# Attention in one decoder block: probabilities turned in 32x32 blocks on VectorE, values on eight places of TensorE's array, three engines in a written order

## The chip, the cores and the metric

The kernel runs on one core of one Trainium2 chip. The metric is device time in microseconds (us), from the start of the execution to its end; the time of a kernel is the median of three runs.

## What is computed

One layer of a hybrid decoder on x of 512 tokens by 1024 channels, in float32. An RMS norm and one input projection feed a sparse-attention mixer, an RWKV-7 mixer and two merge gates; each mixer's result is projected, both are added under sigmoid gates, one more projection and the residual follow, then a gated MLP with a short causal convolution. The change concerns the attention mixer: 8 query heads of 64 in 2 groups (g) that share keys and values, with three branches. At this size all eight blocks of 64 keys are selected and the window of 512 covers all earlier keys, so the selected and the window branch are both plain causal attention, each with keys and values of its own.

```python
s_c = einsum('bsgrd,bcgd->bgrsc', q, kc) + bias_c          # 31 compressed keys
p_c = masked_softmax(s_c, dist_c >= 0, axis=-1)
o_cmp = einsum('bgrsc,bcgd->bsgrd', p_c, vc)
...
sc = einsum('bcgrd,bgcnld->bgrcnl', q_b, k_sel) + bias     # selected keys
p = masked_softmax(sc, mask, axis=(-2, -1))
o_slc = einsum('bgrcnl,bgcnld->bcgrd', p, v_sel)
...
sc = einsum('bqgrd,bkgd->bgrqk', q_b, kw) + bias           # window keys
p = masked_softmax(sc, mask, axis=-1)
o_win = einsum('bgrqk,bkgd->bqgrd', p, vw)
gt = sigmoid(gate)
o = gt[..., 0:1] * o_cmp + gt[..., 1:2] * o_slc + gt[..., 2:3] * o_win
merged = sigmoid(gate_a) * (o @ w_proj_a) + sigmoid(gate_b) * (o_b @ w_proj_b)
```

## The kernel before

**Products in split form.** Dense projections multiply float32 numbers as high and low parts: `hi*hi + hi*lo + lo*hi`, three matmuls for each 128 rows of the contraction. Weights stream through three buffers: `wload` (L258-271) issues a 512 KB load on SP's queue into `raw`, three tiles ahead of use, and `wsplit_` (L282-306) makes `whi` on ScalarE and `wlo` (L300), on VectorE or, for some tiles that the list of weights marks, on GpSimd.

**Names.** `mm` (L122) is a matmul, `act` (L125) a ScalarE activation, `tt`, `ts`, `stt` (L128 to L137) VectorE operations. PSUM has eight banks of 128x512 float32: four of `ps_mm`, two of `ps_a`, two of `ps_b`.

**The attention stage** (L1088-1281) comes when queries (`qst`), keys (`KH` and `KL`, high and low parts) and values (`vt`, 128 tokens on the partitions) stand in SBUF. Its units are a tile of 128 queries (qt from 3 down to 0), a group g and a branch b (0 selected, 1 window); for qt 1 and 0 one unit holds both branches. Since attention is causal, a unit of tile qt has 128*(qt+1) keys for each of 4 heads. For each unit:

- `scores` (L1175-1203): for each PSUM bank of 512 columns two matmuls into `ps_a`; then for each row of heads, VectorE adds the bias and takes the maximum in one instruction (L1196, the name CUSTOM_DVE_ANT_0 in the profile), and ScalarE takes the exponential with its sum (`sm`). The probabilities lie in P, queries on the partitions, in four buffers (`Pb`) that the units use in turn.
- `scale` (L1205-1218): VectorE's reciprocal of the sums, times the gate; then each row of P times its factor, on VectorE, one row in four on ScalarE (qt 3 to 1).
- `turns` (L1221-1233): values need keys on the partitions. For each block of 128 keys TensorE turns four 128x128 pieces (L1231) into one PSUM bank, and `evac` (L1134-1141) copies the bank to SBUF (`PTs`), alternately on ScalarE and VectorE (L1139).
- `values` (L1235-1258): for each 128 keys two matmuls of 128 rows (the keys) by 64 columns (the value channels) with 256 columns of queries stream through the array's two column halves, into a bank `Ob` that adds up both branches. After the last branch ScalarE copies it to `oaT` as high part, and VectorE subtracts for the low part.

`compressed` (L1143-1166) makes the branch with 31 compressed keys for a query tile, all eight heads: one matmul for each head with 64 columns, 32 with the high and 32 with the low part of the keys, which VectorE adds up, then the softmax; `compressed_t` (L1168-1173) turns the result on TensorE (L1172) and `values` multiplies it too.

Between these, `filler(n)` puts n matmuls (128x512) of dense projections, of which 120 are left for this stage: the last merge gates (from `hh`, `hl`) and the RWKV mixer's projection (from `obT`), each tile ended by an activation or by `stt` (L1110-1117). `nfill` says how many stand behind each unit's scores.

**What sets the order.** In this stage only TensorE's instructions run in the order in which they are written (`KTS` holds PE alone). VectorE's and ScalarE's order comes from the scheduler. Ahead of this stage `fill_chain` (L907-923) computes the first merge gates (`siga`, `tb`) by copies out of PSUM; the tanh that makes sigmoids of them is applied in the attention stage (L1111, L1115). After it, `w_proj_a` tiles multiply `oaT` from L1293 on.

## Time and profile before

| | us |
|---|---|
| three runs | 826.81, 826.79, 826.78 |
| median | 826.79 |
| profiled execution | 826.71 |
| its span, from the first to the last instruction | 825.0 |
| attention stage, in the span | 297.77 to 391.99 |

Of the page's part 2, four rows of the span in 40 slices of 20.6 us each; a digit is the busy share of a slice in tenths. The attention stage is slices 14 (its second half) to 18 when they are counted from 0.

```
DVE  6577789975465878797855566665566555323222
ACT  6776655454455777785334554444444444212220
PEclk9999999999999999999999999999999999999999
DMA  8432222246373310001374043333332333323421
```

How to read it: a timeline's row has the start in the span, the duration, the engine, the line, the operation with its output and inputs, the tile of the array (rows * columns) for a matmul, the shape, and the count of alike instructions that stand together. A group's row has busy time and mean duration in ns of one, then the idle time ahead of them. A row of the view by kinds has the least, mean and greatest duration in ns and where in the span they lie. A row of a window has its ends, its length, the busy time of PE, DVE, ACT and POOL with the count of instructions, the granted clock, the DMA share and GB/s. Durations of pipelined instructions overlap, so the distance from start to start says more of what one occupies.

### The profile page before, as it was taken

The numbers are of one execution on the slowest core, as the hardware profiler recorded it, in microseconds if no ns is written. First come the engines' busy times: TensorE is split into PE (matmuls) and PEld (weight loads), VectorE is DVE, ScalarE is ACT, GpSimd is POOL, SyncE is SP. The second block draws the span as 40 slices with busy tenths as digits, with TensorE's granted clock in tenths as the row PEclk, the third lists the DMA queues.
The fourth block names the chain that finished last, engine by engine and source line by source line (L and its number), as shares of the span: only waits on it lengthen the run. The fifth ranks groups of instructions, "written<-read, shape, count | busy, mean of one in ns | idle before, by whom it ended". The sixth has DMA issues, their size and how long they took to land.

```text
span 825.0 us, 12869 instructions
## 1 busy us (share of the span) xinstructions
PE 818.9 (99%) x5087; PEld 668.8 (81%) x5087; DVE 514.1 (62%) x1008; ACT 405.8 (49%) x794; POOL 50.8 (6%) x68
## 2 busy tenths in 40 slices
PE   8999999999999999999999999999999999999998
PEld 7777788987777887887888988888888888888887
DVE  6577789975465878797855566665566555323222
ACT  6776655454455777785334554444444444212220
POOL 6100020140000200110000000000000000000000
PEclk9999999999999999999999999999999999999999
DMA  8432222246373310001374043333332333323421
GB/s 243 110 83 64 77 77 78 71 128 187 103 129 78 86 44 15 26 27 39 106 252 128 2 127 102 92 90 101 102 102 88 91 102 103 99 85 111 141 76 52
DMA packets 109256, 78.66 MB, mean 95 GB/s; under 512 B 3861, under 2 KB 97868, under 8 KB 109196
## 3 DMA queue, kind: packets, MB, share of 16 engines
q1 hardware_dynamic: 106800, 73.92, 31.3%
q10 hardware_dynamic: 1052, 2.48, 0.9%
q0 software_dynamic: 1344, 1.45, 0.9%
q8 instruction: 40, 0.66, 0.3%
q14 instruction: 20, 0.16, 0.1%
HBM read 74.49 MB, written 2.29 MB: 93 GB/s over the span
## 4 chain that ended last, share of the span: by engine, by line
PE 98%; DVE 1%; ACT 1%; DMA 0%; issue 0%; ACTq 0%
PE ps_mm L122 86%; PE ps_a L122 5%; PE ps_b L122 2%; PE ps_b L1231 1%; PE ps_mm L1231 1%; DMA xt<-in_x_dram 0%; PE ps_b L568 0%; PE ps_b L537 0%; PE ps_a L1034 0%; PE ps_a L204 0%; PE ps_a L898 0%; PE ps_b L204 0%; DVE h L132 0%; PE ps_mm L342 0%; ACT P L125 0%; DVE P L1196 0%
## 5 line engine op out<-in xcount | busy, mean ns | idle before, releaser
L300 DVE TENSOR_TENSOR wlo<-raw,whi 128x1024 fp32r<-128x1024 f32 (+1 forms) x111 | 131.5, 1186 | 184.7 <-PE ps_mm L122 160.0
L122 PE MATMUL ps_mm<-hh,whi 128*128 128x512 f32 (+1 forms) x624 | 242.5, 391 | 0.3 <-DVE hl L137 0.3
L122 PE MATMUL ps_mm<-hl,whi 128*128 128x512 f32 (+1 forms) x624 | 240.3, 387 | 0.0
L125 ACT ACTIVATE whi<-raw 128x1024 fp32r<-128x1024 f32 (+3 forms) x124 | 123.2, 995 | 157.4 <-PE ps_mm L122 143.0
L122 PE MATMUL ps_mm<-hh,wlo 128*128 128x512 f32 (+1 forms) x624 | 152.0, 384 | 0.0
L122 PEld LDWEIGHTS ps_mm<-hh,whi 128*128 128x128 f32 x624 | 117.2, 188 | 27.1 <-issue 1.0
L122 PEld LDWEIGHTS ps_mm<-hl,whi 128*128 128x128 f32 x624 | 117.3, 188 | 23.0 <-issue 1.0
L122 PEld LDWEIGHTS ps_mm<-hh,wlo 128*128 128x128 f32 x624 | 115.1, 188 | 23.5
L122 PE MATMUL ps_mm<-whi,aT 128*128 128x512 f32 (+1 forms) x352 | 83.6, 387 | 0.0
L122 PEld LDWEIGHTS ps_mm<-whi,aT 128*128 128x128 f32 x352 | 65.5, 188 | 14.1 <-issue 0.4
L137 DVE SCALAR_TENSOR_TENSOR cgv<-ps_mm,cw,cgv 128x511 f32<-128x511 f32 (+1 forms) x88 | 65.4, 746 | 1.6
L125 ACT ACTIVATE cgv<-ps_mm,cw 128x512 f32<-128x512 f32 x44 | 34.3, 781 | 23.2 <-PE ps_mm L122 23.2
L122 PE MATMUL ps_mm<-wlo,aT 128*128 128x512 f32 (+1 forms) x176 | 43.9, 387 | 0.0
L125 ACT ACTIVATE aT<-cgv 128x512 fp32r<-128x512 f32 x22 | 13.9, 631 | 56.8 <-DVE cgv L128 56.8
L125 ACT ACTIVATE P<-P,nm 128x512 f32<-128x512 f32 (+3 forms) x64 | 35.4, 554 | 11.2 <-DVE nm L1196 10.9
L122 PEld LDWEIGHTS ps_mm<-wlo,aT 128*128 128x128 f32 x176 | 32.8, 188 | 6.7
L125 ACT ACTIVATE cgv<-cgv 128x512 f32<-128x512 f32 x22 | 13.9, 632 | 41.6 <-DVE cgv L137 41.6
L300 POOL TENSOR_TENSOR wlo<-raw,whi 128x512 fp32r<-128x512 f32 (+3 forms) x13 | 20.9, 1608 | 196.1 <-PE ps_mm L122 142.6
L1196 DVE CUSTOM_DVE_ANT_0 P<-ps_a,AB 128x512 f32<-128x512 f32 (+3 forms) x64 | 29.3, 484 | 1.8 <-PE ps_a L122 1.5
L128 DVE TENSOR_TENSOR aT<-cgv,aT 128x512 fp32r<-128x512 f32 x22 | 15.2, 693 | 14.7 <-ACT aT L125 14.7
L128 DVE TENSOR_TENSOR x<-x,ps_mm 128x512 f32<-128x512 f32 (+1 forms) x17 | 10.9, 654 | 20.9 <-PE ps_mm L122 18.5
L125 ACT ACTIVATE QK<-ps_mm 128x64 f32<-128x64 f32 (+5 forms) x56 | 14.8, 308 | 17.7 <-PE ps_mm L122 17.6
(363 smaller groups left out, 1198.4 us busy)
## 6 DMA issues: line engine op xcount, KB each, us to landing
raw<-in_w_up_dram SPq DMA_DIRECT2D x44, 512.0 KB, 3.8
raw<-in_w_in_dram SPq DMA_DIRECT2D x38, 512.0 KB, 3.9
raw<-in_w_down_dram SPq DMA_DIRECT2D x22, 512.0 KB, 3.6
raw<-in_w_out_dram SPq DMA_DIRECT2D x8, 512.0 KB, 4.3
xt<-in_x_dram SPq DMA_DIRECT2D x4, 512.0 KB, 4.6
raw<-in_cmp_w_v_dram SPq DMA_DIRECT2D x4, 512.0 KB, 3.7
raw<-in_w_proj_b_dram SPq DMA_DIRECT2D x8, 256.0 KB, 2.8
raw<-in_w_proj_a_dram SPq DMA_DIRECT2D x8, 256.0 KB, 2.7
```

The source lines that it names most:

```text
L122: te.matmul(o, lhsT=l, rhs=r, start=start, stop=stop)
L125: sc.activation(o, i, f, **kw)
L128: v.tensor_tensor(o, a, b, op=op)
L137: v.scalar_tensor_tensor(o, a, s, b, op0=op0, op1=op1)
L300: low = eng.tensor_tensor(lo, raw, hi.bitcast(F32), op=ALU.subtract)
L1196: maxima.append(v.tensor_tensor_reduce(out=P[:, i], in0=o, in1=BT[:, h, 384 - 128 * qt:512], scale=-1.0, scalar=-NEG, op0=ALU.add, op1=ALU ...
L1231: te.transpose(pt[:, 128 * i:128 * i + 128], P[:, 4 * x + i, 128 * k:128 * k + 128], ident)
```

## The change

1. **Turns on VectorE.** TensorE's transposes and the copies out of PSUM go. Each scaled block of P is turned in place by VectorE (`v.transpose`), which turns every 32x32 piece of it where it stands: the 32 queries of a partition group then lie on the columns, and 32 keys on the partitions of that group.
2. **Values on eight places.** With 32 queries' keys on 32 partitions, a matmul uses 32 rows by 64 columns of the array: four row groups (i, 32 queries each, with a PSUM bank `Oq[i]` each) times two column groups (g). The values must stand in each of the four row groups: `vt` is stored to DRAM (`vs`), behind the gates' factors on ScalarE's queue, and loaded back as replicas, `Va` (8 blocks of 32 keys) and `Vb` (24), by twelve loads on SP's queue, 2 MB together; the compressed values by eight small loads on GpSimd's queue. Groups g are now the innermost loop of the units, so that both groups of a branch multiply together (`values(pair)`).
3. **Compressed branch.** High and low parts are added up by TensorE: two matmuls of 32 columns for each head instead of one of 64, and one addition fewer on VectorE. Its result is turned on VectorE too.
4. **A written order on TensorE, VectorE, ScalarE and SP.** The stage is 44 slots, one for each PSUM bank of scores: maxima, turns of blocks that were scaled at least two slots earlier (one, for the last units), factors, exponentials, then one scaled block; after a slot the scores of the next, values, fillers. Scaling goes to ScalarE; from unit 10 on the even rows of a block go to VectorE.
5. **Fillers** write into the two `ps_b` banks, and their closing operations are put off to the next slot (`later`, `work_off`). The tanh of the gates stands in the copies out of PSUM, ahead of this stage too.
6. `w_proj_a`'s rows come in the order group, head, so each tile is loaded by two DMAs; four copies and four subtractions make `oaT` of a query tile (`outputs`).

The diff, cut to what is spoken of:

```diff
         for m in range(KT):
-            yield cols(A["w_proj_a"][0], 128 * m, NH2)
+            src, *rest = cols(A["w_proj_a"][0], 128 * m, NH2)
+            yield src.rearrange("(g h d) n -> g d h n", g=2, d=DH), *rest
...
-            nc.sync.dma_start(raw, src.rearrange("(k p) n -> p k n", p=128))
+            if len(src.shape) == 4:
+                for g in range(2):
+                    nc.sync.dma_start(raw[64 * g:64 * g + 64], src[g])
+            else:
+                nc.sync.dma_start(raw, src.rearrange("(k p) n -> p k n", p=128))
...
+        sc.dma_start(vs.rearrange("(t p) c -> p t c", p=128), vt.rearrange("p t b c -> p t (b c)"))
...
-            act(siga[m], (yield from dense_fm_g(hh, hl)))
+            act(siga[m], (yield from dense_fm_g(hh, hl)), AF.Tanh, scale=0.5)
...
+    Oq, db = [mmb() for _ in range(4)], [pb(), pb()]
     nd = [0]
+    later = []
+
+    def work_off(n=1, bank_=None):
+        while later and (n > 0 or any(x is bank_ for x, _ in later)):
+            later.pop(0)[1]()
+            n -= 1
 
...
-            act(siga[m], siga[m], AF.Tanh, scale=0.5)
             if m + NGB < KT:
-                act(tb[m + NGB], (yield from dense_steps(hh, hl, KT)))
+                p = yield from dense_steps(hh, hl, KT)
+                later.append((p, functools.partial(act, tb[m + NGB], p, AF.Tanh, scale=0.5)))
                 yield
-            act(tb[m], tb[m], AF.Tanh, scale=0.5)
-            stt(tb[m], tb[m], 1.0, (yield from dense_steps(obT[:, 0], obT[:, 1], NH2)), ALU.add, ALU.mult)
+            p = yield from dense_steps(obT[:, 0], obT[:, 1], NH2)
+            later.append((p, functools.partial(stt, tb[m], tb[m], 1.0, p, ALU.add, ALU.mult)))
...
+    def replicas(k):
+        for i in range(4):
+            qi = slice(32 * i, 32 * i + 32)
+            if k == 0:
+                nc.sync.dma_start(Va[qi], vsb[0, :, 0:8])
+                for g in range(2):
+                    nc.gpsimd.dma_start(vcr[qi, g], vcb[64 * g:64 * g + 32, 2 * g])
+            elif k == 1:
+                nc.sync.dma_start(Vb[qi, 0:8], vsb[0, :, 8:16])
+            else:
+                nc.sync.dma_start(Vb[qi, 8:24], vsb[1])
+
...
-            mm(pc[:, j, g, e], qst[:, h, qs], KC[:, g], True, True)
...
+            for a in range(2):
+                mm(pc[:, j, g, e], qst[:, h, qs], KC[:, g, a], a == 0, a == 1)
...
+        v.transpose(sCs[qt], sCs[qt])
...
+    units = [(qt, (b,), g) for qt in (3, 2) for b in range(2) for g in range(2)]
+    units += [(qt, (0, 1), g) for qt in (1, 0) for g in range(2)]
...
+    def scale(t):
+        if scalable:
+            ui, k = scalable.pop(0)
+            qt, bs, _ = units[ui]
+            n, w = places(ui)
+            N = 128 * (qt + 1)
+            P = Pb[ui % 4][:, n * w * k:n * w * k + n * w]
+            for x in range(n * len(bs)):
+                c = n * len(bs) * k + x
+                row = P[:, N * x:N * x + N]
+                if x % 2 or qt and time_[0] < 10:
+                    act(row, row, AF.Copy, scale=sums[ui][:, c:c + 1])
+                else:
+                    ts(row, row, sums[ui][:, c:c + 1], None)
+            turnable.append((t, P))
+
+    def turns(t):
+        while turnable and turnable[0][0] <= t:
+            P = turnable.pop(0)[1]
+            v.transpose(P, P)
...
+            v.tensor_tensor_reduce(
+                out=P, in0=sp[:, N * x:N * x + N], in1=BT[:, 4 * g + c // B, 384 - 128 * qt:512],
+                scale=-1.0, scalar=-NEG, op0=ALU.add, op1=ALU.min, accum_out=nm[0][:, c:c + 1])
+            rows.append((P, c))
+        turns(t - (2 if ui < 8 else 1))
+        factors()
+        for P, c in rows:
+            act(P, P, AF.Exp, scale=-1.0, bias=nm[0][:, c:c + 1], accum_out=sums[ui][:, c:c + 1])
+        if n > 1:
+            summed.append((ui, n * B * k, n * B * k + n * B, [(ui, k)]))
+        elif k == 3 or k == 1 and ui > 7:
+            f = 2 if ui > 7 else 4
+            summed.append((ui, B * (k + 1 - f), B * (k + 1), [(ui, x) for x in range(k + 1 - f, k + 1)]))
+        scale(t)
+        if ui > 9:
+            scale(t)
...
+    def values(pair):
+        qt, bs, _ = units[2 * pair]
+        B, N = len(bs), 128 * (qt + 1)
+        T = [Pb[(2 * pair + g) % 4][:, 0:4 * B * N].rearrange("p (r b n) -> p b r n", r=4, b=B) for g in range(2)]
+        for y, b in enumerate(bs):
+            for j in range(N // 32):
+                for g in range(2):
+                    for i in range(4):
+                        qi = slice(32 * i, 32 * i + 32)
+                        mm(Oq[i][64 * g:64 * g + 64, 0:128].rearrange("p (r n) -> p r n", n=32),
+                           vblock(b, j)[qi, 64 * g:64 * g + 64], T[g][qi, y, :, 32 * j:32 * j + 32], b + j == 0, False)
+                yield
+        if bs[-1] == 1:
+            sv = sCs[qt].rearrange("p (j g n) -> p g j n", j=2, g=2)
+            for g in range(2):
                 for i in range(4):
...
+                    qi = slice(32 * i, 32 * i + 32)
+                    mm(Oq[i][64 * g:64 * g + 64, 0:128].rearrange("p (j n) -> p j n", j=2), vcr[qi, g], sv[qi, g],
+                       False, True)
+            yield
+
+    def outputs(qt):
+        for i in range(4):
+            act(oaT[:, 0, :, 128 * qt + 32 * i:128 * qt + 32 * i + 32],
+                Oq[i][:, 0:128].rearrange("p (r n) -> p r n", n=32))
+        for i in range(4):
+            qs = slice(128 * qt + 32 * i, 128 * qt + 32 * i + 32)
+            tt(oaT[:, 1, :, qs], Oq[i][:, 0:128].rearrange("p (r n) -> p r n", n=32), oaT[:, 0, :, qs].bitcast(F32),
+               ALU.subtract)
+
...
+    nfill = [[3, 4, 4, 4], [3, 3, 3, 2], [2, 2, 2, 2], [2, 2, 0, 0], [2, 3, 2, 3], [2, 2, 0, 0],
+             [2, 3, 2, 3], [2, 2, 0, 0], [3, 3, 3, 3], [2, 2, 0, 0], [6, 6], [6, 4]]
+    comp = {}
+    with tc.manual_schedule(engines={mybir.EngineType.PE, mybir.EngineType.DVE, mybir.EngineType.Activation,
+                                     mybir.EngineType.SP}):
+        replicas(0)
+        order = [(ui, k) for ui in range(12) for k in range(4 // places(ui)[0])]
+        score(*order[0])
+        t_ = 0
+        for ui in range(12):
+            if ui in (0, 3, 6, 8):
+                comp[0] = compressed({0: 3, 3: 2, 6: 1, 8: 0}[ui])
+            S_ = 4 // places(ui)[0]
+            for k in range(S_):
+                slot(ui, k)
+                work_off()
+                if len(order) > t_ + 1:
+                    score(*order[t_ + 1])
+                t_ += 1
+                if ui == 0 and k == 0:
+                    ob_parts(NT - 1)
+                next(comp[0], None)
+                if ui in (6, 10) and k == 1:
+                    outputs({6: 3, 10: 2}[ui])
+                if ui % 2 and 3 <= ui < 11:
+                    pieces((ui - 3) // 2, (0, 0, 8, 100)[k])
+                filler(nfill[ui][k])
+                if ui == 11:
+                    pieces(4, (8, 100)[k])
+                if ui == 1 and k == 3:
+                    replicas(1)
+                    replicas(2)
+        factors()
+        while scalable:
+            scale(0)
+        turns(100)
+        outputs(1)
         filler(100)
+        work_off(100)
+        pieces(5, 100)
+        outputs(0)
```

## The prediction

> **What bounds the kernel now.** I read the page's first part, then the busy time in the attention stage alone, then that stage by groups, then single stretches of the timeline.

> ```profile
> PE 818.9 (99%) x5087; PEld 668.8 (81%) x5087; DVE 514.1 (62%) x1008; ACT 405.8 (49%) x794; POOL 50.8 (6%) x68
> 297.77:391.99 94.22, 93.99 (x642) 73.84 (x641) 78.22 (x281) 69.64 (x193) 10.34 (x8) 1.00 0.09 26
> ```

> TensorE has no gaps anywhere. The second line is the stretch that the change rewrites, from the first compressed score (297.77) to the first projection of the attention output (391.99): 94.22 us, TensorE 93.99, VectorE (DVE) 78.22, ScalarE (ACT) 69.64, GpSimd 10.34, granted clock 1.00, DMA share 0.09. So TensorE sets the end, but VectorE has only 16 us to spare: the point of the whole prediction.

> **What leaves TensorE and what comes.** These are the groups of that stretch that the change touches, and timelines from which the distance from start to start is read (durations overlap).

> ```profile
> L1231 PE MATMUL ps_b<-kc,P 128*128 128x128 f32 x96 | 13.1, 279 | 0.0
> L1231 PE MATMUL ps_mm<-kc,P 128*128 128x128 f32 x64 | 8.6, 273 | 0.0
> L122 PE MATMUL ps_mm<-PTs,vt 128*64 128x256 f32 x160 | 19.9, 387 | 0.0
> L122 PE MATMUL ps_mm<-sC,kc 128*64 128x128 f32 x64 | 4.9, 273 | 0.0
> L122 PE MATMUL ps_a<-KC,qst 128*128 128x64 f32 x32 | 3.9, 267 | 0.0
> ```
> ```profile
> 297.77 0.98 PE L122 MATMUL ps_a<-KC,qst 128*128 128x64 f32 x8
> 298.58 0.48 PE L122 MATMUL ps_a<-KH,qst 128*128 128x512 f32 x1
> ...
> 309.18 1.04 PE L1231 MATMUL ps_mm<-kc,P 128*128 128x128 f32 x8
> 309.97 0.48 PE L122 MATMUL ps_a<-KH,qst 128*128 128x512 f32 x1
> ```
> ```profile
> 313.39 0.62 PE L122 MATMUL ps_mm<-obT,whi 128*128 128x512 f32 x2
> 313.94 1.95 PE L122 MATMUL ps_mm<-PTs,vt 128*64 128x256 f32 x16
> 315.72 0.61 PE L122 MATMUL ps_mm<-sC,kc 128*64 128x128 f32 x8
> 316.26 0.55 PE L1231 MATMUL ps_b<-kc,P 128*128 128x128 f32 x3
> ```
> ```profile
> 190.73 0.23 PE L122 MATMUL ps_b<-M,AR 64*64 64x64 f32 x2
> 190.75 0.22 PE L122 MATMUL ps_a<-M,AR 64*64 64x64 f32 x2
> 190.79 0.22 PE L122 MATMUL ps_b<-M,AR 64*64 64x64 f32 x2
> ```

> - Removed: 160 transposes at 0.10 to 0.11 us (eight from 309.18 to 309.97), 17 us, and the eight of the compressed branch, 0.9.
> - Values today: 16 passes take 1.78 us, two column halves at once, so a pair has 0.22; 160 passes are 17.7 us. Eight places: the last fence shows four places of 64x64 at once, a round of four each 0.06 us for 64 columns, so about 1.1 columns a nanosecond in every place. With 128 columns a round is 0.11, and a 32-key block of both groups needs two (two passes per matmul: the row of 160 stands for 80 of the code): 0.22. There are 80 such blocks: 17.6. Bounds: nothing dearer if places run beside each other; twice that, +17.6, if only four of the eight do. I take 17.6, by the rows with four.
> - Compressed values: 0.41 for eight passes (the rest of 0.54 is the way out), 3.3 in all, become eight short rounds, 0.5: -2.8.
> - Compressed scores: the 64 columns of a head were one matmul at 0.10 (eight from 297.77 to 298.58); they become two, whose weight load is as long: 16 x 0.11 = 1.8 instead of 0.8, four times: +3.9.
> - Changing over to placed matmuls costs 0.1 each way (313.94 is 0.55 after 313.39, where two matmuls of 0.23 would take 0.46); there are 11 stretches of them after, 12 before.

> TensorE's work so falls by about 17, to 77 us. Were it still the bound, that would be the gain.

> **What VectorE and ScalarE get.**

> ```profile
> L1196 DVE CUSTOM_DVE_ANT_0 P<-ps_a,AB x64: 239/465/692, 299.3 to 380.0; 128x512 f32<-128x512 f32 x16, 128x384 f32<-128x384 f32 x16, 128x256 f32<-128x256 f32 x16, 128x128 f32<-128x128 f32 x16
> L125 ACT ACTIVATE P<-P,nm x64: 386/554/729, 300.1 to 381.6; 128x512 f32<-128x512 f32 x16, 128x384 f32<-128x384 f32 x16, 128x256 f32<-128x256 f32 x16, 128x128 f32<-128x128 f32 x16
> L132 DVE TENSOR_SCALAR P<-P,sm x52: 277/351/490, 306.4 to 383.9; 128x128 f32<-128x128 f32 x16, 128x512 f32<-128x512 f32 x12, 128x384 f32<-128x384 f32 x12, 128x256 f32<-128x256 f32 x12
> L125 ACT ACTIVATE P<-P,sm x12: 495/618/733, 305.8 to 369.0; 128x512 f32<-128x512 f32 x4, 128x384 f32<-128x384 f32 x4, 128x256 f32<-128x256 f32 x4
> L1139 DVE COPY PTs<-ps_b x12: 677/686/694, 309.4 to 388.0; 128x512 f32<-128x512 f32 x12
> L125 ACT ACTIVATE PTs<-ps_b x12: 576/594/598, 310.4 to 387.5; 128x512 f32<-128x512 f32 x12
> 297.77:391.99 94.22, 6.44 (x72) 5.00 (x72) 11.19 (x25) 3.16 (x8) 1.00 0.09 26
> ```
> ```profile
> 307.62 0.68 DVE L1196 CUSTOM_DVE_ANT_0 P<-ps_a,AB 128x512 f32<-128x512 f32 x1
> 308.23 0.08 DVE L1196 DVE_READ_ACCUMULATOR2_ANT nm<- 128x1 f32 x1
> 308.23 0.69 DVE L1196 CUSTOM_DVE_ANT_0 P<-ps_a,AB 128x512 f32<-128x512 f32 x1
> ```
> ```profile
> 305.84 0.71 ACT L125 ACTIVATE P<-P,sm 128x512 f32<-128x512 f32 x1
> 306.45 0.71 ACT L125 ACTIVATE P<-P,nm 128x512 f32<-128x512 f32 x1
> 307.07 0.18 ACT L125 ACTIVATION_READ_ACCUMULATOR P<-P,nm 128x1 f32 x1
> 307.16 0.62 ACT L125 ACTIVATE whi<-raw 128x512 fp32r<-128x512 f32 x1
> ```

> The last two fences give what an instruction occupies: on VectorE its duration less 0.07, so a maximum is 0.61 for 512 columns and, by the range 239 to 692 ns, 0.21 for 128; on ScalarE an exponential with its accumulator 0.71 (128: 0.38) and a scaling 0.61 (128: 0.29).

> The new operation is the turn in place. The trace has it only with strides, on one side (the first row) or both (the second):

> ```profile
> L620 DVE STREAM_TRANSPOSE inv<-AB 32x1024 f32<-32x1024 f32 x4 | 8.1, 2027 | 0.0
> L748 DVE STREAM_TRANSPOSE sg<-inv 32x1024 f32<-32x1024 f32 x2 | 4.5, 2243 | 0.1
> L128 DVE TENSOR_TENSOR sg<-QK,prm 128x248 f32<-128x248 f32 x8 | 5.7, 757 | 0.0
> L128 DVE TENSOR_TENSOR sC<-sC,ps_a 128x256 f32<-128x256 f32 x4 | 1.7, 420 | 0.0
> ```

> One strided side gives 2.0 ns a column, that is 1.0 us for 512: the upper end. The lower end is the scaling of 512 columns on VectorE, 490 ns, 0.41 occupied. The last two rows show that stride alone nearly doubles an ordinary operation (248 columns 757 ns, 256 dense ones 420), so a dense turn should come near a dense copy of as many columns: 0.61, and 0.475 for 384. I take these. [...]

> Turned are 20480 columns (40 x 512): 28 turns of 512 and 16 of 384, 24.7 us, and four of 256. Leaving VectorE: 17 copies (17 x 0.61 = 10.4) and 40 of 52 scalings (about 12), of which all go to ScalarE but twelve short ones; that in turn loses 23 copies (23 x 0.49 = 11.3).

> **The order.** All three engines now follow a written order of 44 slots: maximum of slot t, a turn of a block scaled two slots earlier, the factors; exponentials, then a scaling; TensorE the scores of t+1, values, then some of 120 filler matmuls (0.23). Behind a maximum that waits stand the turns, and values wait for those; behind an exponential that waits stands a scaling. TensorE can lead by one slot only, for scores have two banks. Probabilities have four buffers, and each fourth unit's first maximum waits for the values of the unit that had its buffer. So I add up slot by slot, with the costs above, 2.8 us of VectorE for each compressed tile (11.19 / 4; the dropped addition and the new turn balance), eight blocks of values 1.96 with changeover, 0.6 for a filler's closing VectorE operation, 0.52 for a weight split on ScalarE. Slot 1 of unit 3: VectorE 0.61 + 0.61 + 0.6 + 1.1 = 2.9, TensorE 0.9, ScalarE 2.1; slot 2: TensorE 0.46 + 1.96 = 2.4, VectorE 2.1. By units:

> | unit | PE | DVE | ACT | longest of each slot, summed |
> |---|---|---|---|---|
> | 0, 1, 2 | 7.1, 4.4, 3.7 | 5.8, 4.0, 5.2 | 4.2, 6.3, 5.3 | 7.5, 6.3, 5.5 |
> | 3, 4, 5 | 8.4, 3.8, 6.5 | 8.5, 4.6, 5.0 | 6.1, 4.8, 5.0 | 10.4, 5.0, 8.0 |
> | 6, 7, 8 | 5.6, 5.5, 6.4 | 8.3, 4.1, 9.4 | 6.4, 4.5, 6.8 | 9.7, 6.2, 10.4 |
> | 9, 10, 11 | 6.0, 3.7, 6.9 | 5.7, 6.5, 5.8 | 7.0, 6.3, 5.3 | 7.7, 7.1, 6.9 |

> Engine sums are 68, 73 and 68, yet the longest engine of each unit sums to 82.2 and the longest of each slot to 90.7. The first score (0.5) and the end come on top: 16 fillers 3.7, the last values 2.1, and 1.2 in which TensorE waits for the four output copies, since no filler is left: 7.5. So 89.7 if engines even out within units, 98.2 if not at all. With a lead of one slot I take a third of the way: 92.5 against 94.22, -1.7. The profiled execution took 826.71 us (span 825.0), so 825.0; the median of the runs is 826.79, 0.08 more, and I leave that aside.

> **Costed at nothing.**

> ```profile
> raw<-in_w_in_dram SPq DMA_DIRECT2D x38, 512.0 KB, 3.9
> ```

> Twelve SP loads of value replicas (2 MB), the values' store ahead of them, and two loads instead of one for each of eight projection tiles: the first replica has over 20 us, the second about ten for 0.5 MB, against 3.9 for such a load, at a DMA share of 0.09. Uncovered, each microsecond late is one on TensorE. Weight loads behind them on SP lead by three tiles. Eight small loads on GpSimd's queue stand ahead of its splits; the first split has 10 us. Tanh with the gates' copies removes ScalarE work ahead, where TensorE is the bound.

> **Rivals.**
> - *Even flow.* VectorE's 73 plus its 5.6 at the end, 78.5, with the first score and the last values uncovered, about 83: 815.5. For it: ScalarE and TensorE have less to do. Against: the table's alternation. 0.15.
> - *Dear turns (slower).* At 1.0 per 512 VectorE gets 40 x 0.4 = 16 more, some 10 on the path where it is the longest: 102, so 834.5. It is slower than before once a turn of 512 occupies about 0.68. For it: the only rows of the operation. Against: the strides. 0.18.
> - *More waiting.* The slots don't even out and each handover adds a little: 98 to 100, 831 to 833. 0.14.
> - *A lower clock.* The row of the stage has 1.00, without gaps. In the slots behind the table TensorE's longest lack of work is 2.4 us (unit 10, slot 1: VectorE 4.3, TensorE 1.9). [...] 0.03. [...]
> - *Four places, not eight*: +14, 839; the rows with four at full pace speak against. 0.04.
> - The forecast, 822 to 830.7: 0.46. That the turns stay on TensorE is excluded by the instruction order.

> **How the numbers follow.** About 0.2% (1.65 us) is what a measurement can tell from no change. Faster: even flow and six tenths of the forecast's band, 0.43; within: three tenths, 0.14; slower: the rest, 0.43. 816 to 836 leaves out the ends of even flow and dear turns and the four places, about 0.17.

> **What would show it.** Turns of 512 at about 0.69 us; rounds of eight places 0.11 apart; TensorE idle 15 to 20 us in the stage, waiting for VectorE at scores and first values, VectorE waiting for TensorE at units 4, 6, 8; everything outside within 1 us. Wrong if turns take a microsecond, or if TensorE stays without gaps.

## The result: slower, by 1.2%

| | median us | runs | ratio to before, 95% interval |
|---|---|---|---|
| before | 826.80 | 826.78 to 826.89 | |
| changed | 836.17 | 834.68 to 841.37 | 1.0124, 1.0079 to 1.0170 |
| forecast | 825.0 | range 816 to 836 | |

Two things are new besides the time. The runs of the changed kernel lie 6.7 us apart, those of before 0.1; and the mean granted clock is no longer 1.00: 0.986 in the profiled execution (841.37 us, span 839.6), 0.989, 0.992 and 0.996 in the others, the shorter time always with the higher clock.

From the page of the changed kernel, busy time and the granted clock in 40 slices (slices 15, 16 and 18, counted from 0, have 8 tenths; in before every slice had 9):

```profile
PE 816.9 (97%) x6071; PEld 667.6 (80%) x6071; DVE 518.7 (62%) x1007; ACT 402.2 (48%) x799; POOL 54.5 (6%) x76
...
PEclk9999999999999998898999999999999999999999
```

The attention stage of the same execution, from the first score to the first projection of its output:

```profile
299.03:406.77 107.74, 92.72 (x1625) 73.10 (x1623) 83.64 (x281) 74.08 (x213) 11.86 (x12) 0.89 0.21 49
```

107.74 us, where before took 94.22 and the forecast had 92.5. TensorE is busy for 92.7 of it, with gaps, at a clock of 0.89. The stage starts 1.3 us later; what follows it takes as long as before (432.8 against 433.0 us). This is the slowest of the four executions, 5.2 us above their median. The trace of e5_again, the same kernel at 834.05 us, has this row for the stage:

```profile
298.88:399.53 100.65, 87.06 (x1625) 67.52 (x1624) 82.90 (x281) 74.32 (x213) 11.93 (x12) 0.95 0.23 53
```

TensorE's idle time, 15.0 us in the first and 13.6 in the second, is at or a little under what the prediction expected (15 to 20). What is longer than expected is its busy time, 92.7 and 87.1 us where the prediction had 77. The groups that the forecast priced (mean ns of one behind the busy time):

```profile
L1230 DVE STREAM_TRANSPOSE P<-P 128x512 f32<-128x512 f32 x28 | 19.4, 702 | 1.8 <-ACT P L125 1.6
L122 PE MATMUL ps_mm<-P,Vb 32*64 32x128 f32 x832 | 14.8, 276 | 1.0 <-issue 1.0
L122 PE MATMUL ps_a<-KC,qst 128*128 128x32 f32 x64 | 10.2, 305 | 0.9 <-DVE nm L1260 0.9
L1230 DVE STREAM_TRANSPOSE P<-P 128x384 f32<-128x384 f32 x16 | 9.0, 570 | 0.1
```

A turn of 512 takes 702 ns: the disputed price was right. So the loss lies elsewhere. Four things in the views bear on it.

**The clock halves in fixed stretches.** In the stage the granted clock is either 1 or 0.5, and it changes only at points 3.413 us (or a multiple) apart. These are rows of the windows view cut at those points; the last three columns are clock, DMA share, GB/s:

```profile
312.31:315.72 3.41, 3.32 (x13) 2.10 (x12) 2.79 (x10) 3.41 (x9) 1.15 (x1) 1.00 1.03 226
315.72:319.13 3.41, 1.99 (x11) 1.10 (x9) 3.25 (x7) 3.41 (x10) 0.14 (x1) 1.00 1.23 184
319.13:322.55 3.42, 3.42 (x16) 3.23 (x16) 1.63 (x6) 3.27 (x8) 0.00 (x0) 0.50 1.03 198
322.55:325.96 3.41, 3.41 (x39) 2.33 (x45) 3.23 (x8) 1.33 (x3) 0.32 (x1) 0.50 0.00 0
...
343.03:346.44 3.41, 1.52 (x48) 1.10 (x34) 0.75 (x5) 1.32 (x3) 0.00 (x0) 1.00 0.00 0
346.44:349.85 3.41, 3.41 (x18) 3.41 (x17) 1.28 (x4) 1.21 (x3) 0.00 (x0) 0.50 0.02 5
...
356.68:360.09 3.41, 1.89 (x22) 1.20 (x30) 3.38 (x10) 2.24 (x7) 1.28 (x1) 1.00 0.14 42
360.09:363.51 3.42, 3.42 (x129) 3.09 (x114) 1.54 (x6) 2.61 (x7) 0.00 (x0) 0.50 0.15 41
...
387.40:390.81 3.41, 1.70 (x13) 0.88 (x12) 3.39 (x17) 2.67 (x13) 0.20 (x1) 1.00 0.28 82
390.81:394.23 3.42, 2.47 (x96) 2.47 (x100) 3.38 (x18) 3.42 (x15) 0.86 (x1) 0.50 0.00 0
```

Each fall of the clock comes right after a stretch in which TensorE did little, though its longest gap there was only 0.8 to 1.9 us. PE's busy time (1.5 to 2.0) overstates what it did, since a matmul's record reaches past its columns: a filler of 512 columns is recorded with 0.39 us, but the next starts 0.23 after it. Counted by columns at this distance (what overlaps counted once), TensorE streamed for 0.30, 0.26, 0.39 and 0.31 of these four stretches. The full speed returns after a stretch that is well filled (0.67 and more, in the last section).

**TensorE runs out of instructions.** Inside a run of values it stops, here two matmuls before the end, and the profile shows nothing that it waits for (`issue`):

```profile
342.73 0.65 PE L122 MATMUL ps_mm<-P,Vb 32*64 32x128 f32 x27
...
343.19 0.45 PE L122 MATMUL ps_mm<-sC,sq 32*64 32x128 f32 x11
345.54 0.37 PE L122 MATMUL ps_mm<-sC,sq 32*64 32x128 f32 x2 [1.89 <-issue]
```

The DMA view of the same stretch, 342.6 to 345.6 in 40 slices of 0.075 us, shows one packet, which starts in the second slice, on the queue that carries instructions:

```profile
DMA  0900000000000000000000000000000000000000
...
q8 instruction: 1, 0.02, 2.8%
```

From 342.7 to 345.54 are 2.8 us. The two other gaps of this sort (329.04 and 340.95) end 2.7 and 2.65 us after the start of such a packet. In the stage there are 13 of them, where before had 5 (that view over each stage, the changed kernel first):

```profile
q8 instruction: 13, 0.21, 0.9%
```
```profile
q8 instruction: 5, 0.08, 0.4%
```

A packet is 0.21 MB / 13 = 16 KB. The count goes with TensorE's instructions: the stage's rows have 1625 matmuls and 1623 weight loads with 13 packets, 250 for each; in before 642 and 641 with 5, 257 for each.

**The engines wait for each other.** Waits of TensorE in the stage:

```profile
PE ps_a L122 <- DVE nm L1260: 8.6, 10, 2.6
PE ps_mm L122 <- issue: 2.9, 3, 1.9
```

8.6 us for maxima, whose banks the next scores need.

**A small VectorE operation is longer beside GpSimd.** It clamps the compressed branch's sums; its rows of before and of the changed kernel (least, median, greatest ns), then what stands beside the longest:

```profile
L132 DVE TENSOR_SCALAR mx<-mx x4: 164/168/169, 303.9 to 370.1; 128x8 f32<-128x8 f32 x4
```
```profile
L132 DVE TENSOR_SCALAR mx<-mx x4: 171/478/1011, 305.4 to 372.3; 128x8 f32<-128x8 f32 x4
```
```profile
372.01 1.26 POOL L305 TENSOR_TENSOR wlo<-raw,whi 128x512 fp32r<-128x512 f32 x1 [13.87 <-ACT whi L125]
372.29 1.01 DVE L132 TENSOR_SCALAR mx<-mx 128x8 f32<-128x8 f32 x1
```

It ends with GpSimd's operation, and so does the one of 784 ns, at 326.17; the other two stand beside no such operation and took 171 and 172. The four are 2.1 us long instead of 0.7, and the longest stands in a chain that TensorE waits for at 374.6. The rows show the two operations ending together; what holds the clamp is not shown.

### The profile page after: what moved, and what is told of

Same layout as the page of the kernel before. It is cut to its first block, busy times and chain, and to the rows that moved or that the text cites. A ratio compares the mean times of both kernels' runs of the same rounds, so it can differ in the third digit from the quotient of the medians.

```text
span 839.6 us, 14901 instructions
## 1 busy us (share of the span) xinstructions
PE 816.9 (97%) x6071; PEld 667.6 (80%) x6071; DVE 518.7 (62%) x1007; ACT 402.2 (48%) x799; POOL 54.5 (6%) x76
## 3 DMA queue, kind: packets, MB, share of 16 engines
HBM read 76.59 MB, written 2.82 MB: 95 GB/s over the span
## 4 chain that ended last, share of the span: by engine, by line
PE 89%; DVE 5%; ACT 3%; DMA 2%; issue 1%; POOL 0%; ACTq 0%; POOLq 0%; DVEq 0%
PE ps_mm L122 80%; PE ps_a L122 4%; PE ps_b L122 3%; ACT P L125 2%; DVE P L1260 1%; DVE P L1230 1%; DMA raw<-in_w_in_dram 1%; DMA pra<-in_rwkv_ln_b_dram 1%; POOL pra L166 0%; ACT whi L125 0%; PE ps_b L573 0%; DVE AB L137 0%; DVE sC L128 0%; DVE oaT L128 0%; PE ps_b L542 0%
## 5 line engine op out<-in xcount | busy, mean ns | idle before, releaser
L122 PE MATMUL ps_mm<-hh,whi 128*128 128x512 f32 (+1 forms) x616 | 239.6, 391 | 1.6 <-ACT whi L125 1.2
L122 PE MATMUL ps_mm<-hl,whi 128*128 128x512 f32 (+1 forms) x616 | 237.3, 387 | 0.0
L125 ACT ACTIVATE whi<-raw 128x1024 fp32r<-128x1024 f32 (+3 forms) x124 | 123.2, 995 | 160.3 <-PE ps_mm L122 141.3
L122 PE MATMUL ps_mm<-hh,wlo 128*128 128x512 f32 (+1 forms) x616 | 149.7, 384 | 0.0
L122 PEld LDWEIGHTS ps_mm<-hh,whi 128*128 128x128 f32 x616 | 115.8, 188 | 27.9 <-ACT whi L125 1.7
L122 PEld LDWEIGHTS ps_mm<-hl,whi 128*128 128x128 f32 x616 | 116.0, 188 | 22.6 <-issue 1.0
L122 PEld LDWEIGHTS ps_mm<-hh,wlo 128*128 128x128 f32 x616 | 113.7, 188 | 23.1
L122 PE MATMUL ps_mm<-whi,aT 128*128 128x512 f32 (+1 forms) x352 | 83.7, 388 | 0.0
L122 PEld LDWEIGHTS ps_mm<-whi,aT 128*128 128x128 f32 x352 | 65.5, 188 | 14.0 <-issue 0.4
L125 ACT ACTIVATE cgv<-ps_mm,cw 128x512 f32<-128x512 f32 x44 | 34.2, 779 | 22.9 <-PE ps_mm L122 22.9
L125 ACT ACTIVATE P<-P,nm 128x512 f32<-128x512 f32 (+3 forms) x64 | 35.3, 552 | 18.2 <-DVE nm L1260 17.5
L122 PE MATMUL ps_mm<-wlo,aT 128*128 128x512 f32 (+1 forms) x176 | 43.9, 387 | 0.0
L125 ACT ACTIVATE aT<-cgv 128x512 fp32r<-128x512 f32 x22 | 13.9, 632 | 57.2 <-DVE cgv L128 57.2
L122 PEld LDWEIGHTS ps_mm<-wlo,aT 128*128 128x128 f32 x176 | 32.9, 188 | 6.7
L1260 DVE CUSTOM_DVE_ANT_0 P<-ps_a,AB 128x512 f32<-128x512 f32 (+3 forms) x64 | 29.1, 476 | 10.1 <-PE ps_a L122 6.1
L125 ACT ACTIVATE cgv<-cgv 128x512 f32<-128x512 f32 x22 | 13.9, 632 | 41.0 <-DVE cgv L137 41.0
L125 ACT ACTIVATE P<-P,sm 128x512 f32<-128x512 f32 (+3 forms) x52 | 29.0, 578 | 2.6 <-DVE sm L128 2.6
L1230 DVE STREAM_TRANSPOSE P<-P 128x512 f32<-128x512 f32 (+1 forms) x44 | 28.4, 654 | 1.8 <-ACT P L125 1.6
L122 PE MATMUL ps_a<-KH,qst 128*128 128x512 f32 (+2 forms) x48 | 19.8, 415 | 7.7 <-DVE nm L1260 7.6
## 6 DMA issues: line engine op xcount, KB each, us to landing
raw<-in_w_up_dram SPq DMA_DIRECT2D x44, 512.0 KB, 3.9
raw<-in_w_in_dram SPq DMA_DIRECT2D x38, 512.0 KB, 4.4
raw<-in_w_down_dram SPq DMA_DIRECT2D x22, 512.0 KB, 3.6
raw<-in_w_out_dram SPq DMA_DIRECT2D x8, 512.0 KB, 4.2
xt<-in_x_dram SPq DMA_DIRECT2D x4, 512.0 KB, 4.5
raw<-in_cmp_w_v_dram SPq DMA_DIRECT2D x4, 512.0 KB, 3.8
```

The costliest lines, as they stand in the source:

```text
L122: te.matmul(o, lhsT=l, rhs=r, start=start, stop=stop)
L125: sc.activation(o, i, f, **kw)
L1230: v.transpose(P, P)
L1260: v.tensor_tensor_reduce(out=P, in0=sp[:, N * x:N * x + N], in1=BT[:, 4 * g + c // B, 384 - 128 * qt:512], scale=-1.0, scalar=-NEG, op0=AL ...
```

## Experiments

Each ratio stands against executions of before that were taken beside the run; their medians lie between 826.78 and 827.48 us. Where the clock matters, a run's us at half clock are h = 2 (1 - clock) x span, and the "line" is what the changed kernel's eight executions (four of the result, four of e5_again) give: 830.8 + 0.38 h, correlation 0.93. Single executions lie up to 1.6 us off it, its 830.8 is uncertain by about 1 us (the lowest h is 6.7), and before itself moves by 0.7 us; a distance from the line of under 1 us tells nothing, and one of 2 little more than its sign.

| run | median us | ratio, interval | mean h | mean against the line |
|---|---|---|---|---|
| e5_again | 837.02 | 1.0129, 1.0112 to 1.0146 | 16.3 | (in the line) |
| e1_warm | 838.20 | 1.0132, 1.0115 to 1.0149 | 5.9 | +4.9 |
| e2_mix | 837.18 | 1.0128, 1.0113 to 1.0143 | 15.5 | +0.7 |
| e3_noturn | 828.65 | 1.0018, 1.0006 to 1.0029 | 12.1 | -7.1 |
| e4_kc64 | 834.40 | 1.0092, 1.0071 to 1.0112 | 15.0 | -2.2 |
| e6_fill | 834.64 | 1.0092, 1.0077 to 1.0107 | 5.8 | +1.4 |
| e7_fill_kc64 | 836.71 | 1.0116, 1.0101 to 1.0131 | 8.4 | +2.5 |
| e8_sched | 833.19 | 1.0073, 1.0053 to 1.0093 | 13.3 | -3.0 |
| e9_wide | 832.47 | 1.0060, 1.0045 to 1.0075 | 10.8 | -2.5 |
| e10_narrow | 872.95 | 1.0554, 1.0525 to 1.0584 | 30.5 | +30.8 |
| e11_sched_kc64 | 828.77 | 1.0019, 1.0009 to 1.0028 | 8.1 | -5.0 |
| e12_sched_kc64_mix | 829.24 | 1.0028, 1.0018 to 1.0038 | 8.3 | -4.5 |
| e13_sched_kc64_wide | 832.90 | 1.0059, 1.0041 to 1.0077 | 17.2 | -5.1 |
| e14_sched_kc64_pool | 827.64 | 0.9999, 0.9989 to 1.0009 | 6.6 | -6.0 |
| e15_sched_kc64_fill | 826.50 | 0.9991, 0.9982 to 1.0000 | 5.0 | -6.0 |
| e16_all | 825.21 | 0.9970, 0.9959 to 0.9980 | 3.3 | -7.0 |
| e17_all_mix | 827.94 | 1.0007, 0.9998 to 1.0016 | 7.8 | -5.7 |
| e18_all_store | 825.34 | 0.9981, 0.9972 to 0.9990 | 3.3 | -6.9 |

**e5_again.** No edit. 

> The changed kernel unaltered, beside the three that follow, for its time against its granted clock. Theory A (each halved stretch of 3.41 us costs about half of itself where TensorE sets the pace): the times rise by 0.3 to 0.5 us for each us at half clock, as in its first four runs (834.68 with 6.7, 835.14 with 13.3, 837.21 with 18.4, 841.37 with 23.5), and point to 830 to 832 at full clock. Theory B (the clock fills waits only): no relation to the clock, all within 1.5 us.

Times 834.05, 835.73, 838.31, 838.52 at h = 10.0, 13.3, 20.1, 21.8. Theory A: the time rises with h, by 0.38 us for each us, and the line points to some 831 without it.

The line alone doesn't say which causes which. The two traces of this kernel do: they hold the same instructions, so they can be laid side by side by the starts of VectorE's 64 maxima (L1260).

| maximum, from 0 | changed, us | e5_again, us | later by | at half clock since the row above |
|---|---|---|---|---|
| 0 | 299.69 | 299.54 | 0.15 | |
| 12 | 317.80 | 317.65 | 0.15 | none |
| 17 | 331.54 | 328.94 | 2.60 | changed 6.8 |
| 23 | 338.80 | 336.19 | 2.61 | none |
| 25 | 346.50 | 343.39 | 3.11 | none |
| 27 | 354.46 | 349.91 | 4.55 | changed 6.8, e5_again 3.4 |
| 30 | 359.66 | 355.13 | 4.53 | none |
| 32 | 364.18 | 358.10 | 6.08 | changed 3.4 |
| 39 | 374.00 | 367.92 | 6.08 | none |
| 51 | 382.86 | 378.75 | 4.11 | e5_again 6.8 |
| 56 | 389.57 | 384.60 | 4.97 | none |
| end of the stage | 406.77 | 399.53 | 7.24 | changed 6.8 |

Two steps stand where neither ran at half clock: 0.5 us ahead of maximum 25, where a gap for instructions was 1.89 us in one trace and 1.34 in the other, and 0.9 between 51 and 56. All else moves where one of them ran at half clock longer than the other, by 0.3 to 0.5 us for each such us. So the halved clock makes the executions differ; at the line's 0.38 it also accounts for about half of the loss.

**e1_warm.**

```diff
+    def warm(n):
+        for _ in range(n):
+            te.matmul(Oq[3][:, 128:512], lhsT=qst[:, 0, 0:128], rhs=KH[:, 0, 0, 0:384], start=not open_[0], stop=not open_[0])
...
+                    warm(WARM.get(order[t_ + 1], 0))
                     score(*order[t_ + 1])
```

> The changed kernel with extra matmuls (128x384, into PSUM columns that nobody reads) where TensorE waits ahead of scores and of the last values; nothing else is moved. Theory A (the halved clock is the main loss; its four runs took 834.7 to 841.4 with 7 to 24 us of the span at half clock): the granted clock rises to 0.998 or more and the time falls to 825 to 829. Theory B (the three engines wait for each other slot by slot, and the halved clock only fills time in which TensorE would have waited): the clock rises too, the time stays at 831 or more. If the clock stays at 0.99, the waits are not what lowers it.

The clock rose (0.996 to 0.998), the time didn't fall: theory B. But the extra matmuls have a price of their own: one group of them waited 2.1 us for `oaT` of the tile before. So the run shows that little work lowers the clock; of the time at full clock it says little.

**e2_mix.**

```diff
+            if pair < 4 and x % 4 == 3:
+                filler(1)
...
```

> One filler matmul behind every four 32-key blocks of values (tiles of 512 and 384 keys), taken from the slots around. Theory C (TensorE's instructions run out inside the long runs of short matmuls: three gaps of 0.40, 0.58 and 1.89 us without any wait in the profiled execution): the gaps without a wait shrink from 2.9 us to under 0.5 and the time falls by 2 to 3 at the same clock. Rival: the changeovers between placed and full matmuls (0.2 each time, some 16 more) take back what the gaps give, time within 1 us of the changed kernel at the same clock.

In its trace no gap without a wait is left inside the values of the first four pairs. The time stays on the line (+0.7): the rival.

**e3_noturn.** Leaves out the turns.

```diff
-            P = turnable.pop(0)[1]
-            v.transpose(P, P)
+            turnable.pop(0)
```

> Leaves out the 44 turns of P on VectorE, so values multiply unturned probabilities. 26 us of VectorE work go. If VectorE sets the pace of the stage: 10 to 14 us faster than the changed kernel, 822 to 826. If ScalarE (0.71 for an exponential and 0.61 for a scaling in each slot) and TensorE's low clock set it: 2 to 5 us faster, 831 to 834, and TensorE's waits for maxima stay over half of their 8.6 us.

28.4 us of VectorE work go, 7.1 us of time at a like clock: between the two figures. Even with the turns free, the changed kernel is no faster than before (1.0018). TensorE's wait for maxima falls from 8.6 to 4.2 us, the 2.9 us for instructions stay.

**e4_kc64.**

```diff
-            for a in range(2):
-                mm(pc[:, j, g, e], qst[:, h, qs], KC[:, g, a], a == 0, a == 1)
+            mm(pc[:, j, g, e], qst[:, h, qs], KC[:, g], True, True)
...
+        tt(sC, sC, pcs[:, :, 1], ALU.add)
```

> Part 3 undone: a head's compressed scores are one matmul with 64 columns and VectorE adds the halves. By the prediction's term TensorE gets 3.9 us less (16 x 0.11 to 8 x 0.10, four times) and VectorE 1.7 more. If TensorE is on the path there, since it runs them at half clock (3.1 and 3.3 us for sixteen): 3 to 4 us faster. If VectorE's chain behind them is: 0 to 2 us slower.

-2.2 at a like clock, short of the 3 to 4: part 3 of the change costs, TensorE is on the path there, and saving VectorE one addition isn't worth it.

**e6_fill and e7_fill_kc64.** Other lists `nfill`, e.g. `[[5, 0, 4, 0], [3, 5, 6, 0], [1, 0, 5, 6], ...]` in e6; e7 has a list of its own, the edit of e4, and turns one slot earlier in units 0, 5 and 7 and one later in 8 and 9. 

> The same instructions; only how many filler matmuls stand in each slot changes: fewer where VectorE and ScalarE can run ahead, up to seven where TensorE stood nearly idle, so that TensorE works in over 0.4 of every stretch of 3.4 us. Theory A (the clock falls where TensorE works too little within a stretch, and that costs): granted clock 0.996 or more, 828 to 832. Theory B (VectorE's and ScalarE's order sets the end whatever TensorE does): 833 to 836, at whichever clock.

> Another spread of the fillers, the compressed scores as one matmul of 64 columns for a head with the addition on VectorE, and turns one slot after the scaling in units 0, 5 and 7. Theory A: granted clock 0.996 or more, 825 to 830, 2 us below the run with fillers alone. Theory B: no better than the run with 64 columns alone, 832 to 836.

The clock rose as wanted (h 5.8 and 8.4), the time fell little: e6 has B's figure, e7 lies 0.7 above B's. By its mean e6 won 2.4 us of the 3.8 that the line gives for its clock. Its waits show where the rest may have gone:

```profile
PE ps_a L122 <- DVE nm L1260: 6.1, 11, 1.4
PE ps_mm L122 <- issue: 5.7, 4, 1.9
PE ps_a L122 <- issue: 1.3, 1, 1.3
```

The waits for maxima fell by 2.5 us, those without a releaser rose to 7.0 us instead of 2.9. A likely reason, not tried by itself, is that with fewer fillers around the values and TensorE at full speed a run of values uses up its instructions sooner.

**e8_sched.**

```diff
-    with tc.manual_schedule(engines={mybir.EngineType.PE, mybir.EngineType.DVE, mybir.EngineType.Activation,
-                                     mybir.EngineType.SP}):
+    with tc.manual_schedule(engines={mybir.EngineType.PE, mybir.EngineType.SP}):
```

> VectorE's and ScalarE's order in the stage is left to the scheduler again, TensorE's and SP's stay as written. If the written order is what makes the engines wait: 3 to 6 us faster than the changed kernel. If what each slot costs in its longest engine does: within 2 us of it at the same clock. If the scheduler puts the turns behind later work: slower by 2 or more.

-3.0 at a like clock, at the lower edge of the first figure. Exponentials wait 12.0 us for maxima, where it was 17.5.

**e9_wide and e10_narrow**, the dose of instructions.

```diff
-            for j in range(N // 32):
+            for j in range(0, N // 32, 2):
...
-  Oq[i][..., 0:128], vblock(b, j), T[...][:, 32 * j:32 * j + 32]
+  Oq[i][..., 0:256], vblock(b, j), T[...][:, 32 * j:32 * j + 64]     # e9
+  for e in range(2): ... 64 * e:64 * e + 64, T[...][2 * e:2 * e + 2] # e10
```

> Values with half as many matmuls, each over twice the columns: one matmul for 64 keys' columns with the first 32 keys' values, so the second 32 keys' values are left out and the output isn't attention's; the columns that stream stay the same, 256 weight loads and matmuls of a run become 128. Theory C2 (the array runs out of instructions, 16 KB of which arrive 2.2 to 3.0 us after each request): the gaps without a wait inside values, 3.7 to 6.7 us a run, fall under 1; a run of sixteen blocks takes under 3.7 us; the time falls by 4 to 7 against the changed kernel at a like clock, to 827 to 831. Theory D (columns and the waits between engines): spacing and time stay, within 2 us of it.

> Values with twice as many matmuls, each over two heads (64 columns) instead of four; the sums are the same. Theory C2: the instruction fetches in the stage rise from about 13 to about 23, the gaps without a wait double at least, the time rises by 8 us or more, to 843 or more. Theory D: under 3 us more, since the columns are the same.

Eight blocks of values in e9, then in e10 (a timeline each), and e10's waits:

```profile
337.83 2.03 PE L122 MATMUL ps_mm<-P,Vb 32*64 32x256 f32 x64
339.79 0.44 PE L122 MATMUL ps_a<-KH,qst 128*128 128x384 f32 x1
```
```profile
332.04 0.95 PE L122 MATMUL ps_mm<-P,Vb 32*64 32x64 f32 x44
333.87 1.97 PE L122 MATMUL ps_mm<-P,Vb 32*64 32x64 f32 x128 [0.88 <-issue]
337.32 1.43 PE L122 MATMUL ps_mm<-P,Vb 32*64 32x64 f32 x84 [1.48 <-issue]
```
```profile
PE ps_mm L122 <- issue: 17.0, 15, 1.7
```

In e9 64 matmuls of 256 columns take the 2.0 us that 128 of 128 took, and no wait for instructions is listed. In e10 128 matmuls of half the columns take nearly as long as 128 whole ones (13.8 ns from start to start, where it was 14.4): with so few columns their number doesn't set the distance, so a run takes twice the time. Packets of instructions in the stage rise from 13 to 23 (8 in e9), the wait from 2.9 to 17.0 us. C2 holds in direction. Its size does not: taking the gaps away won 2.5 us at a like clock, not 4 to 7, and e10's +30.8 is more than gaps, since the runs double too.

**e11_sched_kc64 and e12_sched_kc64_mix.** The edits of e8 and e4; in e12 that of e2 as well. 

> Compressed scores as one matmul of 64 columns for a head, and VectorE's and ScalarE's order left to the scheduler. Alone they brought about 2 and 3 us. If they take different waits away: 828 to 831. If both only shift the same wait: 831 to 834.

> The same with one filler behind every four blocks of values. If the instruction fetches are hidden by fillers at less than they cost once TensorE's other waits are gone: 1 to 3 us below the run without them, 826 to 829, no slower than the kernel before. If the changeovers cost as much as the gaps: within 1 us of it or above.

The two add up: -5.0. Mixing in the fillers brings nothing here either.

**e13 to e15**, each one edit on e11: e9's; `nc.gpsimd.tensor_copy(hi, raw)` in the place of ScalarE's copy within the stage; e6's `nfill`. 

> The run with the scheduler's order and the 64-column compressed scores, with half as many value matmuls over twice the columns (every second block of values left out, so the output isn't attention's). If instruction fetches are what is left between that run and the kernel before: 824.5 to 826.5, faster than before. If VectorE and ScalarE set the rest: within 1 us of 828.8.

> The same run with the high parts of the stage's weight tiles copied by GpSimd instead of ScalarE (0.5 us each on ScalarE). If ScalarE's length of a slot counts: 1 to 3 us faster, 826 to 828. If GpSimd's copies hold VectorE up or come too late for the fillers: slower by 1 or more.

> The same run with the fillers spread as in the run with fillers alone. If TensorE's low windows still cost: 1 to 2 us faster, 827 to 828, at a clock of 0.997 or more. If the instruction gaps grow with the denser runs, as they did there: no faster.

In e13 no wait for instructions is left (e11 had 2.5 us), but TensorE waits 13.4 us for maxima instead of 9.6, and h rises from 8.1 to 17.2. In the two traces VectorE's and ScalarE's instructions of the stage stand in the same order by operation, tile and shape. At a like clock e13 lies where e11 does (-5.1 and -5.0): on top of these edits taking the instruction gaps away won nothing, since TensorE waits for VectorE instead and the emptier stretches cost clock. So e9's 2.5 us are no fixed price. e14 and e15 gained about 1 and 2 us; in e15 the gaps for instructions are 5.1 us.

**e16_all and e17_all_mix.** e11 with e6's `nfill` and e14's copies; e17 with a filler behind every four blocks of all tiles as well, taken from the slots. 

> The edits that helped, together: scheduler's order on VectorE and ScalarE, compressed scores as one matmul of 64 columns, fillers spread as in the run with fillers alone, high parts of weights on GpSimd. If ScalarE's splits are on the path besides the low windows: 824.5 to 826, faster than both kernels. If the instruction fetches alone are left: as without GpSimd's copies, 826.5 within 0.5.

> The same with one filler behind every four blocks of values. The gaps without a wait, 5.6 us in the run with the fillers spread, fall under 1.5. If they are what is left: 822.5 to 825. If the changeovers take it back: within 1 us of the run without them.

e16 is faster than both kernels, than before by 0.3%: 0.9970, 0.9959 to 0.9980. Two of its eight executions have a clock of 1.000 (824.18 and 824.64 us). Its waits:

```profile
PE ps_a L122 <- DVE nm L1263: 5.0, 5, 2.3
PE ps_mm L122 <- issue: 4.5, 4, 1.5
```

e17 has no such gap left inside its values and is 2.7 us slower than e16, which neither figure had. The lower clock (h 7.8 against 3.3) gives 1.7 of it by the line; the changeovers are a likely part of the rest.

**e18_all_store.** On e16's kernel; the `dma_start` of `vs` is written behind the gates of `siga`. 

> The run with the edits that helped together, and the store of the values to DRAM issued some tens of us later, ahead of the last gates' columns. Theory (the store, 0.52 MB, stands among 2.25 MB of loads that fill the DMA engines at 0.9 for 8 us, and TensorE waits 1.2 us for the weights behind it at 197): the wait at 197 goes and everything behind it comes 1.2 us earlier, 823.6 to 824.3. If the loads are late for another reason: no change, 825.2.

The DMA view from 186 to 198 still has the store's 0.52 MB, since the scheduler issued it there all the same, and TensorE's wait stays:

```profile
q10 hardware_dynamic: 528, 0.52, 12.4%
```
```profile
PE ps_mm L122 <- ACT whi L125: 0.9, 1, 0.9
```

So the edit did not do what it says, and the cause of the 1.3 us ahead of the stage stays open. The store fits: in this window the changed kernel moves 2.82 MB and the DMA engines stay full up to 198, before moved 2.28 MB and they fell idle at 196.5; but no run took the store away. In the changed kernel the delay is the second of these rows of the timeline, a weight split that came late; before started that matmul at 196.70:

```profile
194.80 1.95 PE L122 MATMUL ps_mm<-raw,sg 128*64 128x256 f32 x16
197.97 0.50 PE L122 MATMUL ps_mm<-hh,whi 128*128 128x512 f32 x1 [1.22 <-ACT whi L125]
```

## Why the prediction was wrong

The step that failed is the one that put TensorE's clock at nothing in the sum (the rival "a lower clock", 0.03), and with it the supply of TensorE's instructions, which the prediction doesn't have at all. The runs show 15.9 us at half clock in the mean, about 6 us of time, and gaps for instructions that e9 prices at 2.5.

- **"A lower clock", 0.03:** the rival that was dismissed. It looked at the longest single lack of work, 2.4 us by its table; in the traces the clock fell after a stretch of 3.413 us in which TensorE streamed for 0.06 to 0.42 of it, and several short gaps make such a stretch (the longest of each was 0.8 to 1.9 us in the changed kernel). Mean h is 15.9 us over the eight executions, at 0.38 each 6 us: half of the 11 to 12 us between forecast and measurement. The price comes from executions of one kernel, the two traces side by side included; e6, which raised the clock by its fillers, won 2.4 us of 3.8.
- **Instruction supply:** not in the prediction at all. The 160 value matmuls of 256 columns became 1280 of 128 (832 on `Vb`, 448 on `Va`); their fetch was not costed. 2.5 us (e9), and nothing on top of e11's edits (e13).
- **"Costed at nothing":** the clamp beside GpSimd (1.4 us in all) and the 1.3 us ahead of the stage. The DMA share of 0.09 was read in the stage; the store runs a hundred us earlier, where the share is 0.92 (190 to 198 in before). The replicas themselves came in time: TensorE's waits name no load of them.
- **Turns, 0.69:** right (702 ns; 570 for 384). The dear turns are refuted. They still cost: 7.1 us of the whole (e3).
- **Rounds of eight, 0.11:** right (128 passes at 14.4 ns: eight in 0.115). Four places are refuted.
- **Compressed scores, +3.9 on TensorE:** the sign right, the size 2.2 in time (e4).
- **"I take a third of the way":** open. By the first maxima of each unit, units 0 to 10 of the execution in e5_again took 7.6, 4.4, 6.1, 9.9, 4.6, 7.8, 11.7, 6.4, 11.5, 7.9 and 7.1 us, 85.0 in all. For them the table's longest of each slot sums to 83.8, its longest engine of each unit to 75.2, and a third of the way is 78.1. So it looks as if the slots didn't even out (the rival "more waiting", 831 to 833, whose time is near the line's 830.8 at full clock). But the 85.0 holds 10.2 us at half clock (3.9 by the line), gaps for instructions inside values (2.0) and the two long clamps (1.5 more than alone). Without these, if they don't overlap, it would be 77.6, an estimate that fits the third. e8's 3.0 us show that the written order costs something; no run shows how far slots even out.

Clock 6, instructions 2.5, clamp 1.4 and start 1.3 make 11.2. That this meets the difference is no proof: the parts overlap, the compressed scores' 1.7 too many count against them, and the clamp and the start were tried by no run.

The saving is there, but small. e16 at a clock of 1.000 stands 3.0 us below the before taken beside it, near the forecast of 825.0. It holds four further edits, of which one takes back part 3 of the change and one the written order on VectorE and ScalarE, so it doesn't bear the forecast out.

## What to carry to other kernels

When work leaves an engine that set the end, look at what it does in each 3.4 us afterwards, not for its longest gap: in these traces, where TensorE streamed under about 0.4 of such a stretch, the next mostly ran at half speed and gave part of the saving back (40 falls, after 0.06 to 0.42; the emptiest that kept full speed had 0.35). Splitting a matmul into small places multiplies the instructions; count them against the supply, here about 250 for each packet of 16 KB, and prefer wide columns where the layout allows (fillers between the values removed gaps, but won no time in e2, e12 and e17). And before a time is laid to a schedule, take out what the clock did to it.
